# Gates of a bidirectional HGRN2 scan, two units at a time as 2x2 blocks with seven block products, and the scan in three groups of units instead of two

## The chip, the cores and the metric

The kernel runs on one core of one Trainium2 chip. The metric is the device time of one execution in microseconds (us); the time of a kernel is the median of several executions. TensorE (PE) multiplies matrices into PSUM, VectorE (DVE) and ScalarE (ACT) work on the elements, GpSimd (POOL) does small operations, and SyncE (SP) issues most of the DMA transfers.

## The reference

One layer: a bidirectional HGRN2 mixer over 2048 latent tokens behind 256 context tokens, then a gated ConvFFN, both behind a normalisation with adaLN. Width 1024, 8 heads of 128. Cut to the part that the change touches:

```
h = modulate(rmsnorm(x), shift, scale)                    # context and latent tokens
q, zf_fwd, zf_bwd, v, g = split(h @ w_in, 5)              # w_in 1024 x 5120
q = silu(q)
for d, zf in enumerate((zf_fwd, zf_bwd)):
    f = lb[d] + (1 - lb[d]) * sigmoid(zf)                 # the gates
    logf[d], k[d] = log(f), 1 - f
# per head and direction, in chunks of 64 tokens:
# S_t = diag(f_t) S_{t-1} + k_t v_t^T,   o_t = S_t^T q_t
y = (rmsnorm(o_fwd + o_bwd) * silu(g)) @ w_out
```

## The kernel before, in words

**Tiles and units.** Tokens go in tiles of 128: two of context (-2, -1) and sixteen latent ones (0 to 15). Three tiles are a unit of 384 tokens. `GROUPS` has two groups of three units. For a group, the normalised and transposed tokens stand in SBUF, in six places; all eight heads are walked over the group's units, then the next group's tokens take the places.

**Products.** Every operand is split into a high and a low part (`split`, L79 to L81: ACT copies the high part, DVE subtracts), and a product is three matmuls for each of eight slices of the inner dimension (`mm3`, L353 to L358: high x high, high x low, low x high). Per head and unit there are the two gates (`z`, 2 x 24 matmuls of 384 columns), the queries (24 of 384) and the values with the output gate (72 of 256); the first unit, with two context tiles, has other forms of the last two. A head's weights are loaded from w_in as five raw tiles of 0.5 MB (`load_feat`, `load_vg`, L162) and split, in each group anew.

**The scan of a unit** (`unit`, L363). The gates pass a sigmoid on ACT and an affine on DVE (L404). DVE makes running products along the chunks: S (L448) forwards, F (L461) backwards, their reciprocal rt (L463), and from these ke, kd, km of the keys and qp, qe, qm, qi of the queries (L453 to L492). The queries' own gate is q (L440). Each value tile's output gate is st (L424): it reads PSUM, so the value's PSUM buffer is free only behind it. Then, for each of three tiles, `part_a` transposes kd (L542, PSUM buffer "tr") and makes four score matmuls (L550 to L557) that DVE masks (L563 to L566), and `part_b` makes kv and o (L574, L589) and updates the state Sf (L593). These six steps are left in a list, and run between the products of the unit that follows.

**Buffers that matter.** In PSUM the ring "pj" has three buffers, for gates, queries and values in turn. "tr" has one, for the transposes of kd and for those of new tokens (`transpose_mod`, L108 to L119: four blocks on PE, L112, then four `hm` on ACT, L116, or DVE, L119). Tokens of the group that follows are loaded into `xt` (two buffers, `x_tile`), normalised (a square L100, a power on POOL L77, a scaling L103) and transposed, all between the products of the last head.

**What sets the order.** The code's lists give the order in which work is issued to the framework, whose scheduler then sets an order for each engine within the dependences; on the chip each engine keeps it. Between the end of the values of one unit and the gates of the next PE has no other work than this. Other work that is spread in between: the rest of w_ada (`ada_rest`) and, in the last head, the eight steps of the output weights (`out_weight`, L642 is DVE's product in it).

The seven block products are not new to the kernel: its ConvFFN has them, in the lines behind L720. After the scan come the readout with w_out and the ConvFFN; the change leaves both alone.

## Time and profile before

| | |
|---|---|
| median of three runs | 2854.65 us (2854.46 to 2859.17) |
| the profiled execution | 2854.57 us |
| its span, first to last instruction | 2852.8 us |
| mean granted TensorE clock | 0.997 of full speed |
| SP loads of w_in | 80 of 0.5 MB, 3.7 us each to landing |
| loads of new tokens (xt) | 11 of 0.5 MB |
| from HBM, to HBM | 280.65 MB, 101.99 MB |

In the trace's names, out<-in tells what an instruction writes and reads; L is the line of the kernel. A timeline row has the start, the duration, the engine, the line, the operation and its tiles, and in brackets for how long the engine stood idle before it and what ended that. Matmuls overlap, so their pace is read from start to start. A row of groups ends with busy time, the mean of one in ns, and idle time before. The scan runs from about 41 to about 1332 us of the span.

### The profile page before, as it was taken

How to read it: one execution, taken by the hardware profiler on the slowest of the kernel's cores; microseconds unless marked ns; L12 is line 12 of the kernel's file. 1: busy time of each engine (PE TensorE's matmuls, PEld its weight loads, DVE VectorE, ACT ScalarE, POOL GpSimd, SP SyncE). 2: the span in 40 equal slices, each digit the busy share in tenths (PEclk: the TensorE clock that was granted, in tenths of full speed). 3: DMA queues.
4: the chain of work that ended last, by engine and by line, in shares of the span. 5: the costliest groups of instructions: out<-in, count | busy, mean ns of one | idle time of the engine just before them, and what ended most of it. 6: DMA issues, size and time to landing. Idle time of an engine off the chain costs nothing. (4 is left out here: it accounts for less than half of the span.)

```text
span 2852.8 us, 43739 instructions
## 1 busy us (share of the span) xinstructions
PE 2803.9 (98%) x16016; PEld 2503.4 (88%) x16016; DVE 2080.8 (73%) x3698; ACT 1176.5 (41%) x2517; POOL 570.1 (20%) x1020
## 2 busy tenths in 40 slices
PE   7999999999999999998999899999999999999999
PEld 4999999999999999998888688888888888887887
DVE  5766666677667566587898787777887777676887
ACT  5433333355333323333555444444444444333343
POOL 2111111121111111111111243433443342000001
PEclk9999999999999999999999999999999999999999
DMA  6222222222232222135778622225522223987663
GB/s 237 67 79 79 84 76 84 79 78 89 85 90 66 80 78 85 61 98 185 266 293 315 227 86 71 88 82 190 187 89 89 76 73 115 310 301 252 194 200 122
DMA packets 202623, 385.51 MB, mean 135 GB/s; under 512 B 26660, under 2 KB 117796, under 8 KB 197160
## 3 DMA queue, kind: packets, MB, share of 16 engines
q1 hardware_dynamic: 199672, 374.46, 39.1%
q10 hardware_dynamic: 2736, 8.26, 0.8%
q8 instruction: 126, 2.06, 0.3%
q14 instruction: 89, 0.73, 0.1%
HBM read 280.65 MB, written 101.99 MB: 134 GB/s over the span
## 5 line engine op out<-in xcount | busy, mean ns | idle before, releaser
L356 PE MATMUL z<-vh,hh 128*128 128x256 f32 (+1 forms) x1024 | 300.3, 293 | 0.0
L358 PE MATMUL z<-vh,hl 128*128 128x256 f32 (+1 forms) x1024 | 293.4, 287 | 0.0
L357 PE MATMUL z<-vl,hh 128*128 128x256 f32 (+1 forms) x1024 | 293.3, 286 | 0.0
L356 PE MATMUL z<-hh,wh 128*128 128x384 f32 x768 | 264.1, 344 | 0.7 <-ACT hh L80 0.7
L357 PE MATMUL z<-hl,wh 128*128 128x384 f32 x768 | 258.4, 336 | 0.5 <-DVE hl L81 0.5
L358 PE MATMUL z<-hh,wl 128*128 128x384 f32 x768 | 258.7, 337 | 0.0
L1338 PE MATMUL y<-wd,ml 128*128 128x512 f32 x600 | 234.0, 390 | 2.1 <-DVE ml L81 2.1
L1336 PE MATMUL y<-wd,mh 128*128 128x512 f32 x600 | 233.8, 390 | 0.9 <-DVE P L1390 0.7
L1337 PE MATMUL y<-wd,mh 128*128 128x512 f32 x600 | 233.5, 389 | 0.0
L356 PEld LDWEIGHTS z<-vh,hh 128*128 128x128 f32 x1024 | 196.3, 192 | 0.0
L357 PEld LDWEIGHTS z<-vl,hh 128*128 128x128 f32 x1024 | 196.1, 191 | 0.0
L358 PEld LDWEIGHTS z<-vh,hl 128*128 128x128 f32 x1024 | 195.8, 191 | 0.0
L81 DVE TENSOR_TENSOR w<-raw,w 128x512 fp32r<-128x512 f32 x180 | 141.9, 793 | 43.1 <-ACT w L80 41.1
L484 POOL COPY TX<-S 128x3 f32<-128x3 f32 x48 | 14.6, 304 | 792.4 <-DVE S L448 792.4
L80 ACT ACTIVATE w<-raw 128x512 fp32r<-128x512 f32 x180 | 111.8, 629 | 141.2 <-PE zd L741 78.6
L81 DVE TENSOR_TENSOR w<-s,w 128x512 fp32r<-128x512 f32 x126 | 122.3, 976 | 49.4 <-ACT w L80 48.6
L424 DVE TENSOR_TENSOR st<-z,st 128x128 f32<-128x128 f32 x127 | 36.5, 287 | 158.7 <-ACT st L423 158.6
L356 PEld LDWEIGHTS z<-hh,wh 128*128 128x128 f32 x768 | 145.3, 189 | 4.4 <-DVE acc L620 1.7
L419 ACT ACTIVATE v<-z 128x128 f32<-128x128 f32 x128 | 35.4, 277 | 271.1 <-PE z L358 271.1
L357 PEld LDWEIGHTS z<-hl,wh 128*128 128x128 f32 x768 | 145.2, 189 | 0.7 <-DVE hl L81 0.7
L358 PEld LDWEIGHTS z<-hh,wl 128*128 128x128 f32 x768 | 144.7, 188 | 0.0
L738 PE MATMUL zc<-rT,w 128*128 128x512 f32 x352 | 137.1, 389 | 2.7 <-ACT w L80 2.7
(337 smaller groups left out, 8119.8 us busy)
## 6 DMA issues: line engine op xcount, KB each, us to landing
raw<-in_w_up_dram SPq DMA_DIRECT2D x88, 512.0 KB, 3.8
raw<-in_w_in_dram SPq DMA_DIRECT2D x80, 512.0 KB, 3.7
lr<-m SPq DMA_DIRECT2D x49, 512.0 KB, 5.5
m<-r SPq DMA_DIRECT2D x66, 256.0 KB, 4.3
raw<-in_w_ada_dram SPq DMA_DIRECT2D x32, 512.0 KB, 4.5
stash<-st SPq DMA_DIRECT2D x125, 128.0 KB, 1.9
kq<-stash SPq DMA_DIRECT2D x15, 1024.0 KB, 7.4
og<-stash SPq DMA_DIRECT2D x15, 1024.0 KB, 6.3
```

The lines of the kernel that those rows point to most:

```text
L80: act.activation(h, src, AF.Copy)
L81: dve.tensor_tensor(l, src, h.bitcast(F32), OP.subtract)
L356: pe.matmul(o, sh[:, k], mh[:, k], start=k == 0, stop=False)
L357: pe.matmul(o, sh[:, k], ml[:, k], start=False, stop=False)
L358: pe.matmul(o, sl[:, k], mh[:, k], start=False, stop=k == KT - 1)
L419: act.activation(v[:, s], z[:, 0:128], AF.Copy)
L424: dve.tensor_tensor(st[:, 1], z[:, 128:256], st[:, 1], OP.mult)
L484: pool.tensor_copy(TX[:, 0, :, 0], tot[:, 0, :, 1])
L738: pe.matmul(o, w[:, 0, k], r[:, :, 0, k], start=start and k == 0, stop=False, skip_group_check=True)
L1336: pe.matmul(z, lh, rh, start=start, stop=False, skip_group_check=True)
L1337: pe.matmul(z, lh, rl, start=False, stop=False, skip_group_check=True)
L1338: pe.matmul(z, ll, rh, start=False, stop=stop, skip_group_check=True)
```

## The change

**Gates.** Two units a and b make a pair. Their gates are one block product: on the left the weights A (rows: the two directions; columns: the two halves of the inner dimension), on the right the tokens B (rows: the halves; columns: a and b). It is done by seven products of half the depth instead of eight, in the order of the tuple `GATES`, with sums S1 to S4 of weight blocks and T1 to T4 of token blocks; ACT and DVE put the seven together in PSUM and SBUF (`gates`: a copy, and additions at L540, L544, L551, L555, L559). Each product is 12 matmuls of 384 columns. The first unit's two gates are complete behind the fourth and the sixth product, the second unit's behind the fifth and the seventh. The first pair of all is done plainly (`gates_plain`). The affine of the gates is on ACT now (L510).

**Three groups of two units.** A group holds eight right factors (B11 to B22, T1 to T4) in SBUF. Those of groups two and three are made beside the heads of the group before (`prep`, spread by `BESIDE` and `weave`), stored to DRAM (fac_d), and loaded when the places come free (`next_factors`). `xt` has one buffer, which the pieces to be stored and the sums of w_ada also use (tag "xt").

**Weights are split once.** A head's seven left factors (wf_d) and its value and query weights (wv_d) are stored after the first group and loaded in the later ones (`prepare`, four products ahead, five buffers; `vq_weights`, one buffer each).

Counted: the 384-column gate matmuls go from 2304 to 2028; raw loads of w_in from 80 to 42; new are 16 stores and 32 loads of 1.5 MB for wv_d, 56 stores and 112 loads of 0.5 MB for wf_d, 48 stores of 0.5 MB and 16 loads of 1.5 MB for fac_d.

The order is moved with it. On DVE, in a unit of the second half before, the queries' products and the first st follow the one unit's scans:

```order
L563 COPY_PREDICATED AB_434<-mx,sc 128x128
L593 SCALAR_TENSOR_TENSOR Sf<-Sf,sd,kv 128x128
L564 COPY_PREDICATED AB_434<-mb,sc 128x128
L565 COPY_PREDICATED AB_435<-mf,sc 128x128
L467 TENSOR_TENSOR qp<-q,F_430 128x384
L566 TENSOR_TENSOR at<-AB_434,AB_435 128x128
L468 TENSOR_TENSOR qp<-q,F_430 128x384
L492 TENSOR_TENSOR qm<-qp,TX_438 128x3x64
L492 TENSOR_TENSOR qe<-qp,rt 128x768
L492 TENSOR_TENSOR qi<-qp,TB_436 128x768
L492 TENSOR_TENSOR qm<-qp,TX_438 128x3x64
L424 TENSOR_TENSOR st<-z,st 128x128
```

On DVE, in a pair of the third group of the change (F_514 is the first unit's, F_515 the second's; L644 and L652 are the scans S and F, L607 is st):

```order
L644 SCALAR_TENSOR_TENSOR S<-F_515,d_511 128x396
L623 TENSOR_TENSOR q<-z,q 128x384
L644 SCALAR_TENSOR_TENSOR S<-F_515,d_511 128x396
L704 TENSOR_TENSOR qp<-q,F_514 128x384
L705 TENSOR_TENSOR qp<-q,F_514 128x384
L682 TENSOR_TENSOR qm<-qp,TX_522 128x3x64
L682 TENSOR_TENSOR qe<-qp,rt 128x768
L682 TENSOR_TENSOR qm<-qp,TX_522 128x3x64
L682 TENSOR_TENSOR qi<-qp,TB_520 128x768
L652 SCALAR_TENSOR_TENSOR F_515<-F_515,d_511 128x396 x2
L654 RECIPROCAL rt<-S 128x24
L607 TENSOR_TENSOR st<-z,st 128x128 x3
```

The second unit's four scans stand ahead of the first unit's st; ahead of these rows, and behind L559, stand the first unit's four scans, rt, one Sf, ke, kd and km.

On SP, at the start of the third group of the change (fB are right factors, v the value and query weights, wf a left factor; wf0S_148 is the fifth product's, since four are loaded ahead):

```order
L437 DMA fB_10587<-fac2B_142 128x3072
L437 DMA fB_10589<-fac2B_143 128x3072
L476 DMA v_10591<-wv_200 128x3072
L476 DMA v_10592<-wv_201 128x3072
L451 DMA wf<-wf0S_148 128x1024
L451 DMA wf<-wf0A_149 128x1024
L451 DMA wf<-wf0S_150 128x1024
```

On SP between two heads before, loads of raw weights stand among the stores of results:

```order
L162 DMA raw<-in_w_in_dram 128x1024
L602 DMA stash_74<-st 128x128
L601 DMA stash_74<-st 128x256
L162 DMA raw<-in_w_in_dram 128x1024
L602 DMA stash_75<-st 128x128
L601 DMA stash_75<-st 128x256
```

Four transfers of 1.5 MB now stand ahead of the left factor there; in the other heads of groups two and three it is the two of v. And on PE, in a head of the first group of the change, where a new tile is transposed (tp):

```order
L118 MATMUL tp<-ident,xt 128x128 x4
L741 MATMUL sc<-qm,km 128x128
L734 MATMUL sc<-qe,ke 128x128
L735 MATMUL sc<-qe,ke 128x128
L740 MATMUL sc<-qp,kx 128x128
L741 MATMUL sc<-qm,km 128x128
L726 MATMUL tr<-ident,kd 128x128 x4
L758 MATMUL kv<-v,kt 128x128 x2
L726 MATMUL tr<-ident,kd 128x128 x2
L758 MATMUL kv<-v,kt 128x128 x2
L487 MATMUL z<-fB_228,wf 128x384
L489 MATMUL z<-fB_228,wf 128x384
```

The scan's transposes tr follow the tile's tp through the same PSUM buffer; before, in the last head, tp stood between rows of value matmuls:

```order
L358 MATMUL z<-vh,hh_466 128x256
L112 MATMUL tp<-ident,xt 128x128 x4
L356 MATMUL z<-vh,hh_466 128x256
L357 MATMUL z<-vl,hh_466 128x256
L358 MATMUL z<-vh,hl_467 128x256
L356 MATMUL z<-vh,hh_466 128x256
```

The diff, cut to its core:

```diff
 GROUPS = (
-    ((-2, -1, 0), (1, 2, 3), (4, 5, 6)),
-    ((7, 8, 9), (10, 11, 12), (13, 14, 15)),
+    ((-2, -1, 0), (1, 2, 3)),
+    ((4, 5, 6), (7, 8, 9)),
+    ((10, 11, 12), (13, 14, 15)),
 )
+SCAN_A = ((8, 15), (4, 18), (4, 18))
+SCAN_B = (12, 22)
+BESIDE = ((3, 4), (4, 6), (0, 0))
...
+    GATES = (("A11", "B11"), ("S2", "T2"), ("S3", "T3"), ("A12", "B21"), ("S1", "T1"),
+             ("A22", "T4"), ("S4", "B22"))
...
+    def left_tile():
+        return wp.tile([128, 2, 4, 128], F32R, name="wf", tag="wf", bufs=5)
...
+                def put(n, src, i=i):
+                    w = xp.tile([128, 2, 4, 128], F32R, name="w", tag="xt", bufs=1)
+                    split(w[:, 0], w[:, 1], src)
+                    sp.dma_start(fac_d[g - 1][n][:, i], w.bitcast(F32))
...
+        def prepare(i):
...
+            w = lefts[i] = left_tile()
+            if ("f", h) in kept:
+                sp.dma_start(w.bitcast(F32), wf_d[h][n])
+                return
...
+        def vq_weights(g, h):
+            if ("v", h) in kept:
+                w = vq_tiles()
+                for v, d in zip(w, wv_d[h]):
+                    sp.dma_start(v.bitcast(F32), d)
+                return w
...
+        def gate(h, u, d, z=None):
...
+            act.activation(v, z, AF.Sigmoid)
+            j = (1 - d) * NH + h
+            act.activation(v, v, AF.Identity, scale=oml[:, j:j + 1], bias=lb[:, j:j + 1])
...
+            for n, (ln, rn) in enumerate(GATES):
+                prepare(i + n + 4)
+                w, r = lefts.pop(i + n), fac[rn]
+                if n == 0:
+                    z1 = pj()
+                    acc_gate(z1, w, r, True, False)
+                    u2 = gp.tile([128, NS, 32], F32, name="u2", tag="S")
+                    act.activation(u2, segs(z1), AF.Copy)
+                elif n == 1:
+                    z2 = pj()
+                    acc_gate(z2, w, r, True, True)
+                    dve.tensor_tensor(u2, u2, segs(z2), OP.add)
...
+                elif n == 5:
+                    acc_gate(z3, w, r, False, True)
+                    dve.tensor_tensor(gate_view(0, 1), u2, segs(z3), OP.add)
+                    gate(h, 0, 1)
+                else:
+                    acc_gate(z2, w, r, False, True)
+                    dve.tensor_tensor(gate_view(1, 0), u2, segs(z2), OP.add)
+                    gate(h, 1, 0)
...
+                ua.early()
+                ua.queries()
+                drain()
+                ua.late()
+                if not head0:
+                    ub = Unit(h, w, 1, units[1])
+                    ub.early()
+                if last:
+                    weave([lambda k=k: out_weight(k) for k in range(KT)], 0, 40)
+                else:
+                    weave(some(BESIDE[g][1]), 0, 24)
...
+                        ua.values(s)
...
+                weave(ua.scan(), *SCAN_A[g])
+                ub.queries()
+                ub.values(0)
+                ub.values(1)
+                drain()
+                ub.late()
+                ub.values(2)
+                if h == NH - 1 and not last:
+                    next_factors(g + 1, ("B12", "B22"))
+                scan_b = ub.scan()
```

`early` holds a unit's S and F scans, rt and POOL's factors, `late` the products of keys and queries; `weave` and `drain` spread listed steps over the products that follow.

653 lines of the change are left out of this document (396 added, 257 removed).

## The prediction

> **What bounds the kernel now.** I read the page first: its span, then the busy shares.
>
> ```profile
> span 2852.8 us, 43739 instructions
> PE 2803.9 (98%) x16016; PEld 2503.4 (88%) x16016; DVE 2080.8 (73%) x3698; ACT 1176.5 (41%) x2517; POOL 570.1 (20%) x1020
> ```
>
> TensorE (PE) is busy for 98% of the span and VectorE (DVE) for 73%. That is an average, so I asked for PE's waits between 60 and 1420 us, which is the scan and the first tiles behind it (columns: total us, times, longest).
>
> ```profile
> PE kv L574 <- DVE Sf L593: 2.9, 5, 0.7
> PE tr L542 <- DVE hm L119: 1.7, 5, 1.0
> ```
>
> These are the largest two that a line of the scan has: PE is hardly ever kept waiting there. So a matmul that goes is worth its whole spacing, and a new wait costs its whole length. The spacing is read from PE's timeline, start to start, since durations of pipelined matmuls overlap.
>
> ```profile
> 600.67 0.60 PE L112 MATMUL tp<-ident,xt 128*128 128x128 f32 x4
> 601.02 0.42 PE L356 MATMUL z<-hh,wh 128*128 128x384 f32 x1
> ...
> 602.17 0.33 PE L356 MATMUL z<-hh,wh 128*128 128x384 f32 x1
> 602.34 0.33 PE L357 MATMUL z<-hl,wh 128*128 128x384 f32 x1
> 602.52 0.33 PE L358 MATMUL z<-hh,wl 128*128 128x384 f32 x1
> ...
> 702.62 0.38 PE L542 MATMUL tr<-ident,kd 128*128 128x128 f32 x2
> ...
> 703.73 0.61 PE L574 MATMUL kv<-v,kt 128*128 128x128 f32 x4
> ...
> 704.98 0.28 PE L356 MATMUL z<-vh,hh 128*128 128x256 f32 x1
> 705.10 0.28 PE L357 MATMUL z<-vl,hh 128*128 128x256 f32 x1
> ...
> 707.50 0.60 PE L574 MATMUL kv<-v,kt 128*128 128x128 f32 x4
> ...
> 708.31 0.36 PE L356 MATMUL z<-vh,hh 128*128 128x256 f32 x1
> ```
>
> A 384-column matmul takes 0.174 us (two take 0.35, from 602.17 to 602.52; 0.174 over a longer row of them), a 256-column one 0.12 and four transposes of a tile 0.35. A tile's part_a (transposes and four score matmuls, 702.62 to 703.73) takes 1.11 us, its part_b (kv and o) 0.81. What DVE needs behind the gates stands in its timeline of the same head.
>
> ```profile
> 700.17 0.98 DVE L461 TENSOR_TENSOR_SCAN F<-F,d 128x396 f32<-128x396 f32 x1
> 701.07 0.27 DVE L463 RECIPROCAL rt<-S 128x24 f32<-128x24 f32 x1
> 701.26 0.29 DVE L492 TENSOR_TENSOR km<-ke,TX 128x192 f32<-128x192 f32 x1
> 703.10 0.96 DVE L492 TENSOR_TENSOR kd<-ke,TB 128x768 f32<-128x768 f32 x1 [1.55 <-PE tr L542]
> 703.98 0.55 DVE L440 TENSOR_TENSOR q<-z,q 128x384 f32<-128x384 f32 x1
> 704.48 0.30 DVE L563 COPY_PREDICATED AB<-mx,sc 128x128 f32<-128x128 uint32 x1
> ...
> 706.11 0.55 DVE L468 TENSOR_TENSOR qp<-q,F 128x384 f32<-128x384 f32 x1
> 706.58 0.35 DVE L492 TENSOR_TENSOR qm<-qp,TX 128x192 f32<-128x192 f32 x1
> 706.85 0.95 DVE L492 TENSOR_TENSOR qe<-qp,rt 128x768 f32<-128x768 f32 x1
> 707.72 0.95 DVE L492 TENSOR_TENSOR qi<-qp,TB 128x768 f32<-128x768 f32 x1
> 708.59 0.35 DVE L492 TENSOR_TENSOR qm<-qp,TX 128x192 f32<-128x192 f32 x1
> 708.86 0.28 DVE L424 TENSOR_TENSOR st<-z,st 128x128 f32<-128x128 f32 x1
> 709.06 0.33 DVE L593 SCALAR_TENSOR_TENSOR Sf<-Sf,sd,kv 128x128 f32<-128x128 f32 x1
> 711.94 0.29 DVE L424 TENSOR_TENSOR st<-z,st 128x128 f32<-128x128 f32 x1 [2.55 <-ACT st L423]
> ```
>
> Start to start: an F scan 0.90 (an S scan has the same size and is taken alike), rt 0.19, kd 0.88, q 0.50, qp 0.47, qm 0.27, qe and qi 0.87, st 0.20. The last row shows the slack: DVE stood idle for 2.55 us before the second st, so it was ahead of PE. One unit's chain fits behind PE; the change puts two units' chains in one place.
>
> **The change part by part.** The sum is made against the profiled execution: 2854.57 us, of which the span is 2852.8; the median of the three runs, 2854.65, is the same within 0.1 us.
>
> *Matmuls removed.* The gates of a pair of units take 84 instead of 96 matmuls of 384 columns, for 23 of the 24 pairs (the first stays plain): 276 x 0.174 = **48.0 us** off PE. As PE sets the pace, all of it counts. The transposes only change place. The five additions that DVE gains per pair at 0.50 (q's row) are 2.5 us against four gate affines that go to ACT.
>
> *The wait behind the last product.* The three PSUM buffers of the ring "pj" are shared by the gates, queries and values. The second unit's queries need the buffer of the first unit's first values, which frees with its st product; in DVE's new order that st stands behind the scans of both units. From the last product: the addition L559 (0.50), four S scans and four F scans (7.20), two rt (0.38), Sf (0.27, as qm), two ke (1.00, as q), two km (0.54), kd 0.88, q 0.50, two qp 0.94, two qm 0.54, qe and qi 1.74, st 0.20: 14.7 us. Beside it PE has the first unit's queries (24 x 0.174 = 4.18), its values (72 x 0.12 = 8.58) and one part_b (0.81): 13.6 us. With about 0.3 for two hand-overs, an estimate (ACT's copy of a value starts 0.2 behind PE's next instruction:
>
> ```profile
> 707.70 0.28 ACT L419 ACTIVATE v<-z 128x128 f32<-128x128 f32 x1 [2.60 <-PE z L358]
> ```
>
> against 707.50), PE waits 1.4 us per pair. The bounds are 0 (a tenth less on DVE) and 3.2 (each instruction at its full duration rather than its spacing: 16.5 us in all). Group 2 and group 3 have 8 pairs each: 16 x 1.4 = **+22.4**. In the first group other work stands between, and I count nothing.
>
> *Stored weights loaded again.* In groups 2 and 3 a head's two value tiles (1.57 MB each) go ahead of the fifth product's left factor (0.52 MB) on SP's queue, and can start only when the last values of the head before are done. Rates and latencies, by a window at the start, and the groups and issues that a tile's preparation has:
>
> ```profile
> 15.00:25.00 10.00, 10.00 (x24) 1.96 (x23) 1.65 (x3) 1.31 (x3) 1.70 (x7) 1.00 1.02 410
> ```
>
> ```profile
> L116 ACT ACTIVATE hm<-tp,B,A 128x128 f32<-128x128 f32 x200 | 74.1, 465 | 65.0 <-PE tp L112 64.1 <-DVE A L224 0.9
> L77 POOL TENSOR_TENSOR rs<-rs,mhalf 128x1 f32<-128x1 f32 x34 | 22.9, 677 | 205.0 <-DVE rs L76 200.8 <-issue 3.6 <-DVE B L698 0.5
> L103 ACT ACTIVATE xt<-xt,rs 128x1024 f32<-128x1024 f32 x11 | 12.7, 1153 | 12.6 <-POOL rs L77 12.6
> L100 ACT ACTIVATE junk<-xt 128x1024 f32<-128x1024 f32 x11 | 11.7, 1060 | 5.0 <-DMA xt<-in_x_dram 5.0
> L642 DVE SCALAR_TENSOR_TENSOR raw<-raw,vec,g 128x1024 f32<-128x1024 f32 x8 | 10.1, 1270 | 0.0
> ```
>
> ```profile
> xt<-in_x_dram SPq DMA_DIRECT2D x11, 512.0 KB, 3.9
> ```
>
> The window's last column is 410 GB/s. A load of 0.52 MB needs 1.3 us of that and landed after 3.9, so about 2.6 is latency. The 3.67 MB take 8.95 us, and land after 9.0 to 11.6; four products (48 x 0.174 = 8.35) and two part_a (2.2) make the factor due at 10.6. The wait lies between 0 and 1.0; I take 0.5, the middle, for 14 heads: **+7**. The page "DMA: Bandwidth & Descriptors" of the Trainium skill (Specifications) limits one core's HBM traffic to about 358 GB/s; the trace moved 410, so the measurement decides. By 358 these loads would be 1.3 us later in each of the 14 heads, an estimate of +18 more.
>
> *Right factors made beside.* A tile's x has one buffer now, and its four-block transposes use the one buffer "tr" that the scan's transposes have too. In four heads of the first group: a transpose of four blocks (0.35) and four hm (1.86) until tr is free, the second transpose 0.35, then the next x: load 3.9, square 1.06, power 0.68, scale 1.15. That is 9.35 us until the third transpose. PE has about 6.7 in between (three part_a 3.3, kv and o 1.7, two transposes 0.7, five gate matmuls 0.9, a value 0.1): 2.7 of wait, 4 x 2.7 = 10.8. The transposes that follow each other behind some 1.7 us of matmuls wait 0.5 more, eight times: 4. Together **+15**, between 0 (the planner's order covers it) and 22 (half the small matmuls run ahead).
>
> *Between groups.* SP loads B12, B22 and the two value tiles (6.3 MB) and then the fifth left factor: 6.82 MB / 410 = 16.6, with latency 19.2, against 10.6 due: 8.6 us; I take 8 at each of the two changes, since the first of these loads may start early: **+16** (0 to 2 x 15, if the stores ahead of them are still running). A wait of this kind has a second price in the clock:
>
> ```profile
> 49.57 1.12 PE L112 MATMUL tp<-ident,x 128*128 128x128 f32 x4 [4.93 <-DVE x L105]
> 50.34 0.67 PE L356 MATMUL z<-hh,wh 128*128 128x384 f32 x1
> ...
> 54.33 0.38 PE L356 MATMUL z<-hh,wh 128*128 128x384 f32 x1
> ```
>
> After 4.93 us without work twelve matmuls took 3.99 us (50.34 to 54.33) instead of 2.09, and the transposes 0.77 instead of 0.35: 2.3 us lost. Two such waits: **+4.6**. The page "TensorE: Matmul & The Clock Gate" of the Trainium skill (Part 1: The HAM clock gate) puts the limit at about 3.4 us without work and the return at as long again of work; the trace agrees on the return (4 us), and shows no wait that tests the limit from below. By it the waits of 2.7 cost no clock, and a little longer ones would cost 2.3 each.
>
> *Start and end.* The wait of 4.93 gets 27 instead of 12 matmuls ahead of it: -15 x 0.174 = -2.6. The eight out_weight steps lie in one pair instead of three units: each 1.27 on DVE and a split of about as much, 20 us; a pair takes PE 52 us (132 matmuls of 0.174, 144 of 0.12, six times part_a and part_b), and DVE's 73% of it (38) and 20 pass that by 6, and with their bunching I take 7.6. Together **+5**.
>
> Sum: -48.0 + 22.4 + 7 + 15 + 16 + 4.6 + 5 = +22: **2877 us**, with its own range 2862 to 2895 (half of the walk's waits either way).
>
> **The rivals.**
>
> *A, on the other side: the scan stays bound by PE.* The place is the stretch between L559 and the second unit's queries. DVE's chain is longer than PE's cover by only 1.4 in 14.7; if it runs a tenth shorter (ACT or POOL take parts earlier, scans start before L559 as the first unit's gates are done by the sixth product) the 22.4 go, and with a DVE that keeps up the 7 and the 15 go too. Then -48.0 + 16 + 4.6 + 5 = -22: **2832 us** (2818 to 2848). For it speaks that DVE idled 2.55 us at this place before; against it that the order puts all eight scans behind L559. The point from which it decides: the waits of a pair, over 23 pairs, below about 1 us.
>
> *B, it cancels.* Half of the walk's 44 us of waits are real: 2877 - 22 = **2855**.
>
> *C, the chain at full durations.* If the rows that follow each other don't overlap as they did, each of the 16 pairs waits 3.2 instead of 1.4: +29, **2906 us** (2895 to 2930). For it: PSUM and SBUF are shared with more traffic from stores and loads; against it: the spacings above are from a busy stretch.
>
> **How the numbers follow.** Forecast 0.42, A 0.30, B 0.10, C 0.18. The range takes A down to 2822 and C up to 2925. About 0.2% (5.7 us) is what a measurement of this kernel can tell from no change. A is faster (0.30), B the same (0.10), the forecast and C slower (0.60).
>
> **What would show it.** Right: in the profile after, the waits list has PE waiting for st at the second unit's queries, some 1.4 us in each pair of groups 2 and 3, for the load of wf, and for xt in the first group; two waits of about 8 us stand at the group changes, with the clock low behind them; PE's share falls to some 96%. Wrong: hardly a wait at L559's stretch and pairs of groups 2 and 3 that are 2.1 us shorter than two units of before (then A), or waits there of 3 us (C), or a wait at an engine that I gave none, ACT above all, which takes the affine and the stores' splits.

## The result, and the profile after

The changed kernel takes 2970.93 us (median of 4 runs, 2966.04 to 2971.84), the kernel before, in the same runs, 2856.91 (2854.46 to 2859.41): a ratio of 1.0396 (95% interval 1.0378 to 1.0414), 114 us slower. I had forecast slower, but by 22 us and not over 2925. First the page of the changed kernel: its span and the busy shares.

```profile
span 2968.4 us, 43955 instructions
PE 2815.1 (95%) x15740; PEld 2492.1 (84%) x15740; DVE 2134.7 (72%) x3776; ACT 1268.4 (43%) x2725; POOL 649.3 (22%) x1020
```

PE has fewer matmuls, is yet busy for longer, and its share fell from 98% to 95%. Where it happened shows in the first matmul of the readout, the first work behind the scan, in PE's timeline of before and then of after:

```profile
1327.12 1.95 PE L858 MATMUL oi<-Sb,kq 128*128 128x128 f32 x16
```

```profile
1442.90 2.50 PE L1120 MATMUL oi<-Sb,kq 128*128 128x128 f32 x10 [4.40 <-DMA kq<-stash]
```

The scan ends 115.8 us later, the whole span 115.6: all of it lies in the scan. So in what follows I compare where the scan ends (1442.9 for the change). Busy time by stretch tells waiting from slowness; the whole scan, before and then after, and under it the scan of after in stretches (seven pairs of the first group, its last head with the change of group, the second group, most of the third). The columns are the stretch, its length, busy time of PE, PEld, DVE, ACT and POOL, the granted clock, and the DMA share and rate.

```profile
41.50:1327.10 1285.60, 1271.17 (x9088) 1253.00 (x9089) 866.51 (x1950) 484.23 (x1425) 197.19 (x593) 1.00 0.26 81
```

```profile
41.50:1442.90 1401.40, 1284.11 (x8841) 1241.64 (x8841) 921.58 (x2036) 577.92 (x1636) 271.28 (x590) 0.97 0.59 211
...
69.30:452.90 383.60, 347.41 (x2312) 332.84 (x2312) 285.81 (x629) 218.15 (x554) 80.86 (x177) 0.97 0.63 231
452.90:522.90 70.00, 51.84 (x306) 48.82 (x305) 38.10 (x86) 22.43 (x61) 9.99 (x26) 0.85 0.87 331
522.90:1016.40 493.50, 456.11 (x3150) 437.93 (x3151) 310.01 (x669) 176.34 (x527) 92.43 (x197) 0.97 0.66 233
1016.40:1400.00 383.60, 373.23 (x2724) 370.56 (x2723) 231.72 (x538) 127.95 (x407) 77.80 (x178) 1.00 0.42 151
```

PE stands idle for 117.3 us of the scan (1401.4 - 1284.1) instead of 14.4: 103 more. It is busy 13 us longer though 48 us of matmuls are gone: what is left takes 61 us more. Part of that is the clock, 0.97 of full speed in the first two groups and 0.85 at the change of group. The record of the granted clock has 119 us at half speed in the whole run, and 22 before; about 94 of the 119 are in the scan, 15 of them on idle time, so half of the other 79, some 40 us, is pace lost; before loses 2 to 3 us in its scan in the same way, which leaves 37. Of the other 24 us most are the edges of the waits. In the rows under e2 the last matmul ahead of a wait is shown for 0.28 us where its neighbours follow 0.12 apart, and the first one behind it is followed after 0.29 instead of 0.174: PE is shown busy there, but 0.25 us of pace are lost, in the mean over the change's waits. The change has 106 waits of 0.05 us and more in the scan and before has 20, so this makes some 21 us.

The third group, which has nothing beside it, runs at full clock and waits little; the loss is in the groups that make something else meanwhile. The waits of PE from the start to behind the scan (total us, times, longest), where before had 2.9 as its largest line of the scan:

```profile
PE z L583 <- DVE st L607: 22.1, 15, 3.3
PE tp L118 <- ACT xt L109: 17.3, 7, 3.5
PE kv L758 <- DVE Sf L766: 7.7, 1, 7.7
PE sc L734 <- DVE AB L749: 6.7, 5, 3.5
...
PE sc L734 <- DVE qe L682: 6.1, 6, 2.3
PE kv L758 <- DVE Sf L777: 5.8, 12, 1.5
PE kv L758 <- DVE Sf L764: 5.3, 4, 1.3
...
PE z L585 <- DMA v<-wv: 5.1, 2, 3.9
...
PE z L487 <- DMA fB<-fac1B: 3.5, 2, 3.1
```

The first line is the wait that I forecast behind the last product, the second the wait for xt. The two lines with DMA are loads at the changes of group, and the 7.7 is a store there (e8). The others are new and short, for VectorE's ordinary steps of the scan (Sf, AB, qe), waits to which the prediction gave nothing.

### The profile page after: what moved, and what is told of

Its sections match the earlier page's. It is cut to its first block, busy times and chain, and to the rows that moved or that the text cites. A ratio compares the mean times of both kernels' runs of the same rounds, so it can differ in the third digit from the quotient of the medians.

```text
span 2968.4 us, 43955 instructions
## 1 busy us (share of the span) xinstructions
PE 2815.1 (95%) x15740; PEld 2492.1 (84%) x15740; DVE 2134.7 (72%) x3776; ACT 1268.4 (43%) x2725; POOL 649.3 (22%) x1020
## 4 chain that ended last, share of the span: by engine, by line
PE 57%; DVE 9%; DMA 8%; POOL 2%; issue 2%; ACT 1%; SPq 0%; DVEq 0%; POOLq 0%; ACTq 0%
PE y L1600 3%; PE y L1598 3%; PE y L1599 3%; PE zc L1000 3%; PE zc L1003 3%; PE zc L1002 3%; PE za L1000 3%; PE zd L1000 3%; PE zd L1003 3%; PE za L1003 3%; PE zd L1002 3%; PE za L1002 3%; PE z L487 2%; PE z L491 2%; PE z L489 2%; PE z L594 2%
## 5 line engine op out<-in xcount | busy, mean ns | idle before, releaser
L594 PE MATMUL z<-v,fB 128*128 128x256 f32 (+1 forms) x1024 | 300.2, 293 | 2.1 <-ACT v L86 2.1
L595 PE MATMUL z<-v,fB 128*128 128x256 f32 (+1 forms) x1024 | 294.6, 288 | 2.9 <-DVE v L87 2.7
L596 PE MATMUL z<-v,fB 128*128 128x256 f32 (+1 forms) x1024 | 293.7, 287 | 0.0
L669 POOL COPY TX<-S 128x3 f32<-128x3 f32 x48 | 31.7, 659 | 939.6 <-DVE S L644 939.6
L594 PEld LDWEIGHTS z<-v,fB 128*128 128x128 f32 x1024 | 195.8, 191 | 5.3 <-ACT v L86 3.5
L595 PEld LDWEIGHTS z<-v,fB 128*128 128x128 f32 x1024 | 195.8, 191 | 4.4 <-DVE v L87 4.4
L596 PEld LDWEIGHTS z<-v,fB 128*128 128x128 f32 x1024 | 195.8, 191 | 0.0
L583 PE MATMUL z<-fB,v 128*128 128x384 f32 (+1 forms) x384 | 133.6, 348 | 22.5 <-DVE st L607 22.1
L83 POOL TENSOR_TENSOR rs<-rs,mhalf 128x1 f32<-128x1 f32 (+1 forms) x50 | 57.2, 1143 | 375.0 <-DVE rs L82 368.0
L1000 PE MATMUL zc<-rT,w 128*128 128x512 f32 x352 | 137.0, 389 | 2.1 <-DVE uv L1485 2.1
L86 ACT ACTIVATE w<-s 128x512 fp32r<-128x512 f32 x126 | 78.4, 628 | 137.2 <-POOL s L1056 76.7
L1002 PE MATMUL zc<-rT,w 128*128 128x512 f32 x352 | 136.9, 389 | 0.0
L1003 PE MATMUL zc<-rT,w 128*128 128x512 f32 x352 | 136.9, 389 | 0.0
L1600 PEld LDWEIGHTS y<-wd,ml 128*128 128x128 f32 x600 | 112.6, 188 | 26.5 <-DVE ml L87 3.2
L585 PE MATMUL z<-fB,v 128*128 128x384 f32 (+1 forms) x384 | 129.7, 338 | 5.1 <-DMA v<-wv 5.1
L1598 PEld LDWEIGHTS y<-wd,mh 128*128 128x128 f32 x600 | 112.6, 188 | 24.9 <-ACT X L1633 1.6
```

Of the source, the lines that this page charges most:

```text
L86: act.activation(h, src, AF.Copy)
L583: pe.matmul(z, wh[:, k], self.tok(k, 0, s), start=k == 0, stop=False)
L594: pe.matmul(z, th, wh[:, k, 0:n], start=k == 0, stop=False)
L595: pe.matmul(z, th, wl[:, k, 0:n], start=False, stop=False)
L596: pe.matmul(z, tl, wh[:, k, 0:n], start=False, stop=k == KT - 1)
L1000: pe.matmul(o, w[:, 0, k], r[:, :, 0, k], start=start and k == 0, stop=False, skip_group_check=True)
```

## The experiments

Most runs stand for a part of the change that is undone or made lighter. The median is against 2970.93, the ratio against the kernel before in the same runs; "behind" is the span less the scan's end (1525.5 in the change, 1525.7 before).

| run | median us | ratio (95%) | scan ends | behind |
|---|---|---|---|---|
| e1_eighth | 3006.12 | 1.0517 (1.0499 to 1.0534) | 1484.4 | 1532.5 |
| e2_st_ahead | 2949.51 | 1.0319 (1.0304 to 1.0334) | 1419.4 | 1529.7 |
| e3_ada_off_dve | 2990.00 | 1.0464 (1.0449 to 1.0480) | 1462.2 | 1527.0 |
| e4_two_x | 2949.15 | 1.0316 (1.0301 to 1.0332) | 1417.0 | 1524.8 |
| e5_ada_spread | 2964.55 | 1.0371 (1.0349 to 1.0393) | 1435.4 | 1529.6 |
| e6_filler | 2977.83 | 1.0418 (1.0397 to 1.0439) | 1445.1 | 1529.1 |
| e7_together | 2932.75 | 1.0262 (1.0243 to 1.0281) | 1403.7 | 1525.3 |
| e8_stores_on_act | 2975.21 | 1.0411 (1.0383 to 1.0439) | 1439.7 | 1525.0 |
| e9_warm_power | 3005.95 | 1.0511 (1.0486 to 1.0536) | 1445.6 | 1562.2 |
| e10_one_scan_more | 2975.91 | 1.0414 (1.0388 to 1.0439) | 1446.9 | 1526.3 |
| e11_no_ada_sums | 2942.84 | 1.0298 (1.0272 to 1.0325) | 1413.6 | 1522.8 |
| e12_together_2 | 2958.34 | 1.0348 (1.0326 to 1.0371) | 1396.1 | 1559.7 |
| e13_no_new_tiles | 2907.09 | 1.0180 (1.0163 to 1.0197) | 1377.0 | 1526.9 |
| e14_four_bytes | 3003.12 | 1.0511 (1.0490 to 1.0532) | 1441.6 | 1559.9 |
| e15_sixty_four_bytes | 2997.72 | 1.0492 (1.0471 to 1.0513) | 1441.6 | 1553.7 |
| e16_row_broken | 2956.80 | 1.0354 (1.0334 to 1.0374) | 1430.6 | 1523.2 |

### The gain and the walk: e2 and e1

e2 moves the second unit's scans behind the first unit's values in the order of the code, so that st no longer stands behind them.

```diff
-                    ub.early()
...
                         ua.values(s)
+                if not head0:
+                    ub.early()
```

> The second unit's scans are issued behind the first unit's values; on DVE the first st then stands ahead of two of the second unit's four scans, 1.8 us earlier. Theory (the wait of the second unit's queries for st is real and is this chain): the third group's pairs go from 53.8 to about 52.5 us, and the whole from 2971 to about 2955 (12 to 19 us less). Rival (the chain only moves: the second unit's kd and part_a are late instead): no change, 2971.

The scan ends 23.5 us earlier. One wait of the third group in the change, with the matmuls beside it, and then a pair of that group (from one rt to the next) in the change and in e2:

```profile
1080.75 0.28 PE L596 MATMUL z<-v,fB 128*128 128x256 f32 x1
1082.27 0.45 PE L583 MATMUL z<-fB,v 128*128 128x384 f32 x1 [1.24 <-DVE st L607]
1082.56 0.34 PE L584 MATMUL z<-fB,v 128*128 128x384 f32 x1
```

```profile
1125.26:1179.02 53.76, 52.52 (x386) 52.15 (x385) 31.98 (x76) 17.62 (x57) 10.94 (x25) 1.00 0.43 155
```

```profile
1122.17:1174.43 52.26, 52.26 (x386) 52.09 (x385) 31.96 (x76) 17.65 (x57) 10.97 (x25) 1.00 0.45 162
```

PE has no idle time in e2's pair: 52.26 us where two units of before, in heads with nothing beside, took 54.4 in the mean. So the 2.1 us per pair are there in the third group, and the wait behind the last product is as deduced. The pair is 1.50 us shorter, for a wait of 1.24: the edges are the rest.

e1 makes the second product twice, so that the eighth one is back.

```diff
                     acc_gate(z2, w, r, True, True)
+                    acc_gate(z2, w, r, True, True)
```

> The second product (S2 by T2) is made twice in each of the 23 pairs, 276 matmuls of 384 columns more, with the same result. Theory (PE sets the pace wherever it isn't waiting, so the seven products did save their 48 us and the loss is elsewhere): 276 x 0.174 = 48 us more, about 3019. Rival (the stretch of the gates is bound by DVE, ACT or the loads, so the eighth product had cost little and the change never saved its 48): 0 to 25 us more.

It cost 41.5 us in the scan of the profiled execution, which is the longest of e1's four (3018.57; the median is 35 us above the change). That it is near the 48 of 23 times 12 matmuls is chance: 28 of the 41.5 are in seven pairs of the third group, twice what the matmuls cost there, and 13 in the sixteen pairs ahead of them, where the matmuls alone are 33. So in the first two groups, where PE waits for others, the eighth product had cost less than its length, and the theory holds for the third group only. There a pair became 58.3 instead of 53.8: 2.1 are the matmuls, 0.95 a longer wait at st (2.19 for 1.24; why it grew I don't know), and 1.5 are the clock: in one pair the wait was cut into about 1.8 and 0.4 by the edge of two clock windows, and this pair took 56.8. In e1's timeline of PE matmuls behind the whole wait run 0.32 apart instead of 0.174, and a table in windows of 3.41 us (the length of the clock record's pieces) shows why.

```profile
1098.46 0.44 PE L584 MATMUL z<-fB,v 128*128 128x384 f32 x1 [2.19 <-DVE st L608]
...
1100.07 0.52 PE L585 MATMUL z<-fB,v 128*128 128x384 f32 x1
1100.39 0.52 PE L586 MATMUL z<-fB,v 128*128 128x384 f32 x1
```

```profile
1096.07:1099.49 3.42, 1.23 (x8) 1.03 (x7) 2.73 (x7) 0.45 (x2) 3.36 (x12) 0.99 0.09 24
1099.49:1102.90 3.41, 3.41 (x13) 3.31 (x12) 0.00 (x0) 0.00 (x0) 0.01 (x1) 0.51 0.00 0
```

All 2.19 us are idle inside one window, and the next window has half the clock.

### The clock: e10 and all the records

e10 makes the first S scan of the second unit twice in the third group, so that the wait grows by a scan.

```diff
-                for d in range(2):
+                for d in (0, 0, 1) if tiles[0] == 13 else (0, 1):
```

> In the third group's eight heads the second unit's first S scan is made twice, with the same result: 0.9 us more of DVE ahead of st, so PE's wait there grows from 1.2 to 2.1 us and nothing else changes. Theory of the clock by windows (a stretch of 3.4 us in which PE idles for 2 us or more is followed by one at half the clock, one with less than 1.5 us is not): 0.9 and some 1.5 us for the clock, pairs of 53.8 become 56 or more in most heads, 16 to 20 us in all. Rival (the clock falls only after 3.4 us without any work): pairs of 54.7, 7 us in all.

The wait grew to 2.09 us and the pairs to 54.6, which is the rival's time: in six of the eight pairs the clock stayed at 1.00. A pair of 54.6 us is 16 windows of 3.41, so the wait meets the windows at the same place each time; the stretches on both sides of that boundary:

```profile
1076.10:1079.51 3.41, 3.02 (x26) 2.81 (x24) 3.41 (x6) 0.80 (x4) 0.39 (x1) 1.00 0.07 20
1079.51:1082.92 3.41, 1.72 (x10) 1.72 (x11) 2.03 (x6) 0.09 (x1) 2.53 (x10) 1.00 0.14 40
1082.92:1086.33 3.41, 3.41 (x25) 3.37 (x24) 0.57 (x3) 0.82 (x3) 0.00 (x0) 1.00 0.02 5
```

The wait is cut into 0.4 and 1.7, and no window falls. So e10 doesn't decide between the two; e1's windows above do, where 2.19 us were enough, and a count does: over the change and the experiments e1 to e13, all windows at full speed from 41.5 us to the end of the scan, by PE's idle time within one.

| idle in a window, us | under 1.5 | 1.5 to 1.7 | 1.7 to 2.0 | 2.0 to 3.4 |
|---|---|---|---|---|
| windows | 5022 | 46 | 67 | 176 |
| followed by half speed | 0 | 5 | 45 | 176 |

Behind the scan two windows with 1.3 and 1.5 us idle fell as well (in e1 and e8), so the limit isn't sharp. It isn't the length of a wait that counts but whether about half of a window is idle. The profile before had shown it already, in the ConvFFN: in its timeline of PE and in two windows, a wait of 2.84 us is followed by half the clock.

```profile
1600.65 0.76 PE L738 MATMUL zd<-rB,w 128*128 128x512 f32 x1 [2.84 <-DVE uv L1219]
```

```profile
1597.24:1600.66 3.42, 0.58 (x4) 0.19 (x2) 3.42 (x7) 1.54 (x3) 0.00 (x0) 1.00 1.05 447
1600.66:1604.07 3.41, 3.41 (x8) 2.73 (x9) 0.45 (x1) 0.00 (x0) 0.00 (x0) 0.50 0.93 394
```

And its wait of 3.42 us at 1332.48, which an edge cuts (1.9 and 1.8 us idle in the two windows), is followed by none. The page "TensorE: Matmul & The Clock Gate" of the Trainium skill (Part 1: The HAM clock gate) has the free-running window of 3413 ns, and these records agree; it asks for about 3.4 us without work for the fall, and there the measurement decides: from 2.0 us within one window the clock fell every time.

e6 was to test this the other way: twelve matmuls without a use ahead of the second tile's transposes, to fill the wait for xt.

```diff
+        for _ in range(fill):
+            pe.matmul(tp[:, 0, :], ident, ident, start=True, stop=True)
```

> Before the transposes of each second tile, twelve matmuls of the identity by itself go into their own PSUM buffer, with no effect on the result: PE works for some 2.6 us in a wait of 3.4 that it has anyway, in six heads. Theory (the waits of 3.4 us also halve the clock for 3.4 to 6.8 us, and a shorter stretch without work doesn't): the four long pairs of the first group fall by 1.5 to 3 us each, the whole by 6 to 15 us, though more matmuls run. Rival (the clock is low for other reasons): 0 to 10 us more.

The waits of 3.4 us stayed as they were, since they belong to the first tile's transposes, not the second's: a miss, which tells nothing of the clock, but shows that my place for the xt wait was wrong.

### The wait for xt: e4, e9 and e16

e4 gives the second tile of a head a buffer of its own, so that the chain from the second transpose to the next x is gone.

```diff
-                    hms.append([x_tile(xp, t), hm_tile(f"hm{c}")])
+                    hm = hm_tile(f"hm{c}")
+                    flat = hm.rearrange("p k n -> p (k n)")
+                    if c == 0:
+                        xt, junk = x_tile(xp, t), flat
+                    else:
+                        xt = x_tile(xp, t, xt=flat)
```

> A second tile's x is loaded into its own hm buffer, at the same time as the first one's, instead of after the first one's transposes. Theory (the third transpose waits 3.4 us for its x in four heads of the first group and two of the second, and each of these waits also halves the clock for 3.4 to 6.8 us): 4 x (3.4 + 3) and 5 more, 30 us less, about 2940. Rival (the wait alone counts, and the clock is low for other reasons): 17 us less, about 2954.

The scan ends 25.9 us earlier and the waits for xt fall from 17.3 to 7.8 us in total, but one of 3.4 is left. This is not the chain from the second transpose: in the first group no wait for xt of the change is at a second tile, all are at a head's first one. In the change the wait of this kind in PE's timeline, and the power that the tile's scaling needs, on POOL:

```profile
207.01 1.11 PE L118 MATMUL tp<-ident,xt 128*128 128x128 f32 x4 [3.36 <-ACT xt L109]
```

```profile
202.25 3.53 POOL L83 TENSOR_TENSOR rs<-rs,mhalf 128x1 f32<-128x1 f32 x1 [9.53 <-DVE rs L82]
218.06 0.54 POOL L83 TENSOR_TENSOR rs<-rs,mhalf 128x1 f32<-128x1 f32 x1 [12.28 <-DVE rs L82]
```

One column takes 3.53 us at one place and 0.54 at another. It is slow at 202.25, 308.35 and 412.76, in three of the heads, and the waits of 3.4 are there. In e4 they stand at other places of VectorE's work: two of the three powers take 0.54 and their waits are 0.50, and the third takes 3.53 and its wait is 3.37. My first guess was code that must be fetched; e9 makes a power of another column on POOL just ahead.

```diff
+                    pool.tensor_tensor(idle, TBs[1][:, 0, 0, 3:4], mhalf[:, 0:1], OP.pow)
```

> Before each new tile's square, POOL makes one power more, into a tile that nobody reads, right behind its work for the unit before; that is some 9 us ahead of the power that the tile needs. Theory (that power takes 3.5 us in three heads of the first group because POOL has not run one for 90 us, and is the wait of 3.4 us that PE has there): in these heads the power takes 0.5 to 0.9, the wait goes below 1 us, and the clock stays up: 3 x (3 + 2), 10 to 18 us less, about 2956. Rival (the power is slow for what runs beside it, or the wait has another end): 2971, with 3.5 us as before.

The added powers took 0.54, the tile's own still 3.54: not the code. What lies beside it is VectorE's row of the second unit's queries, here the first instruction behind the power's start and the last one, of seven that follow each other:

```profile
202.29 0.55 DVE L705 TENSOR_TENSOR qp<-q,F 128x384 f32<-128x384 f32 x1
...
204.70 0.68 DVE L87 TENSOR_TENSOR wf<-s,wf 128x512 fp32r<-128x512 f32 x1
```

Each reads two SBUF tiles. The row ends at 205.38 and the power at 205.78, 0.40 later; it is 0.39 at the two other places. e16 puts an instruction that reads nothing into that row.

```diff
                 qe = self.qe = gp.tile([128, 2, NS, 32], F32, name="qe", tag="qe")
+                if self.tiles[-1] < 4:
+                    dve.memset(qe[:, 0, s0 * 4:s0 * 4 + 1, 0:4], 0.0)
```

> In the heads of the first group, a memset of four columns is put on VectorE between the second unit's products qp and qm. In the profile of the change the three slow powers on POOL (3.52 to 3.53 us instead of 0.54, at 202.25, 308.35 and 412.76) all start beside a row of VectorE products that read two SBUF tiles each and follow each other without a gap, and all end 0.39 to 0.40 us behind the end of that row; the memset reads nothing and stands 0.5 us behind the power's start. Theory (POOL's power gets no turn at SBUF while VectorE's products of two SBUF tiles follow each other): the power ends some 0.4 us behind the memset's start, so it takes 1.0 to 1.3 us; the wait of PE for xt in these three heads falls from 3.4 to about 1 us, and with the half-speed windows behind it the scan ends 7 to 13 us earlier, at 1430 to 1436. Rival (something else slows the power there, as its place in POOL's own sequence): it stays 3.5 us, the waits of 3.4 stay, and the scan ends within 4 us of 1442.9.

In e16's timelines, the power on POOL, the memset on DVE and the first tile's transposes on PE:

```profile
203.44 0.98 POOL L83 TENSOR_TENSOR rs<-rs,mhalf 128x1 f32<-128x1 f32 x1 [9.54 <-DVE rs L82]
```

```profile
203.97 0.06 DVE L710 MEMSET qe<- 128x4 f32 x1
```

```profile
205.65 0.66 PE L118 MATMUL tp<-ident,xt 128*128 128x128 f32 x4 [0.82 <-ACT xt L109]
```

The power ends at 204.42, 0.45 behind the memset's start, and takes 0.98 us in all three heads; the wait of 3.36 is 0.82, the waits for xt fall from 17.3 to 7.3 us in all, and the scan ends 12.3 us earlier. (The half-speed time of the whole run didn't fall with it, 123 us for 119.) So it is a lock-out by VectorE's unbroken row, and the rival fell. The page "SBUF — State Buffer" of the Trainium skill (SBUF: two separate sides) says that a VectorE instruction with two SBUF inputs and a GpSimd instruction that reads SBUF exclude each other for an instruction's whole length; the trace agrees, and shows that POOL gets no turn between instructions that follow each other either.

### What is made beside the scan: e13, e11, e5 and e3

e13 leaves the preparation of the new tiles out.

```diff
-                    hms.append([x_tile(xp, t), hm_tile(f"hm{c}")])
-                    xt, hm = hms[-1]
-                    normalize(xt, hm.rearrange("p k n -> p (k n)"), xp, on_act=True)
+                    hms.append([None, hm_tile(f"hm{c}")])
+                    pool.memset(hms[-1][1], 1.0)
...
-                    xt, hm = hms[c]
-                    transpose_mod(xt, hm, half, ps, *mods(t), "tr", 1, True)
+                    return
```

> Leaves out the loads, norms and transposes of the new tiles in the first and second group: the right factors of groups two and three are made of ones, with the same sums, splits, stores and loads. Theory (in the first group the new tiles' chain from load to transposes, with the clock behind its waits, is most of what every second pair takes longer): the pairs of 57 to 58 us there fall to about 49, those of the second group by 3 to 5 where tiles were made, 40 to 50 us less, about 2925. Rival (the splits and stores beside, and the weights that are split and stored, make the first group slow): 10 us less.

The scan ends 65.9 us earlier. The first group's seven pairs of e13 stand against the row of 383.60 above:

```profile
69.90:411.53 341.63, 325.16 (x2258) 317.10 (x2258) 287.56 (x622) 178.01 (x467) 70.53 (x178) 1.00 0.69 250
```

42 us less with the clock at 1.00 and 16.5 us idle instead of 36.2, while DVE is as busy as before. So it isn't that DVE has too much to do, but the waits in the heads with new tiles and the clock behind them: those for xt (12 us in these pairs), and four of 1.32 for Sf, four of 0.5 to 0.8 for kt and three for hm, which e13 hardly has. It takes the tiles' loads and their work on ACT and POOL away with them, so it doesn't say which of these delays Sf and kt. Some 8 us of the 65.9 are the transposes' own time on PE (12 tiles, two rows of 0.35 each), which the kernel before spends too.

e11 leaves out the loads and sums of w_ada that are spread over three pairs of the second group.

```diff
-                raw = rawp.tile([128, D], F32, name="raw", tag="raw")
-                sp.dma_start(raw, a["w_ada"][k * 128:(k + 1) * 128, c:c + D])
...
+                if k == 0:
+                    sp.dma_start(acc[i], a["w_ada"][0:128, c:c + D])
```

> Leaves out the products and sums of the rest of w_ada (31 of 32 loads and all 32 DVE steps); the rows that later parts read are made of one slice alone, by the same matmuls at the same places. Theory (the three pairs of 62 to 66 us are long for these steps on DVE and the clock behind the waits they cause): these pairs fall to 55 or 56, 25 to 30 us less in all, about 2943; the kernel before spent nothing on these steps, since PE did not wait for them. Rival (the loads and stores of the second group make it slow): 5 us less at most.

29.3 us less, 20.5 of it in those three pairs (64.9, 62.5 and 65.5 became 58.7, 55.0 and 58.7). The second of them in the change, then in e11:

```profile
775.10:837.60 62.50, 56.48 (x390) 53.57 (x389) 43.00 (x87) 18.78 (x59) 11.88 (x25) 0.97 0.67 219
```

```profile
759.88:814.89 55.01, 54.59 (x390) 52.35 (x389) 32.24 (x77) 18.80 (x59) 10.93 (x25) 1.00 0.46 162
```

PE waits 6.0 us with ten such sums beside (43.0 - 32.2 = 10.8 us of DVE), and 0.4 without, and the clock comes back. The run takes 31 loads away too, but these aren't what PE waits for: in the three pairs of the change its only wait for a load is one of 1.4 us for wf; the others are for DVE and ACT. The sums stand in DVE's order between the three st, each 1.19 us long:

```profile
722.06 0.28 DVE L607 TENSOR_TENSOR st<-z,st 128x128 f32<-128x128 f32 x1
722.26 1.27 DVE L811 SCALAR_TENSOR_TENSOR acc<-raw,sil,acc 128x1024 f32<-128x1024 f32 x1
723.45 0.28 DVE L607 TENSOR_TENSOR st<-z,st 128x128 f32<-128x128 f32 x1
```

e5 spreads the same sums thinner, over the third group too.

```diff
-BESIDE = ((3, 4), (4, 6), (0, 0))
+BESIDE = ((3, 4), (2, 4), (1, 1))
```

> The same steps of the rest of w_ada, on DVE as in the change, but at most six steps of work beside in a pair of the second group and two in one of the third, instead of ten in the second group and none in the third. Theory (ten steps in a pair put 13 us of DVE work among the chain that PE waits for; two steps find room in the 25% that DVE is idle): the three pairs of 62 to 66 us fall to about 56, the third group's rise by 1 to 2 us each, the whole to about 2945 to 2955. Rival (each step costs PE its 1.28 us and the share of clock wherever it lies): 2971, the third group's pairs 3 us longer.

7.5 us less in the scan: the three long pairs fell to 55 to 60, but the pair of the second change of group rose from 59.9 to 67.0 and the third group's to as much as 58.3, and half-speed time rose from 119 to 142 us. So spreading the sums moved most of the loss to other places.

e3 takes the sums off DVE: the product on ACT, the addition on POOL.

```diff
+                    act.activation(raw, raw, AF.Copy, scale=sil[:, k:k + 1])
+                    pool.tensor_tensor(acc[i], acc[i], raw, OP.add)
```

> The 32 steps of the rest of w_ada, which now lie in the second group's last five heads, are scaled on ACT and added on POOL instead of one DVE instruction of 1.28 us each. Theory (these steps stand in DVE's queue between the parts that PE waits for, and each such wait also lowers the clock): those five pairs come down from 60 to 65 us to about 55, the whole to about 2940 (25 to 35 us less). Rival (the second group is slow because of its loads and stores): no change within 5 us.

19.3 us more. The sum on POOL is late for those who need it, as its list of PE's waits shows:

```profile
PE z L818 <- POOL acc L812: 15.5, 3, 6.5
```

So it moved the wait instead of taking it away, and doesn't tell what the sums cost on DVE.

### The change of group: e8

The longest wait, 7.7 us at the first change of group, is no load of a factor. kv waits for Sf, which waits for ACT's copy kb, which waits for a store of the stash (the results that go to DRAM):

```profile
489.83 0.28 ACT L761 ACTIVATE kb<-kv 128x128 f32<-128x128 f32 x1 [6.42 <-DMA stash<-st]
```

e8 puts the last head's stores on ACT's queue, past the loads of factors on SP's.

```diff
-                q_ = act if h == NH - 1 and t > NT - 4 else sp
+                q_ = act if h == NH - 1 else sp
```

> In the last head of each group the stores of results go to ACT's queue, so that they don't stand behind the loads of right factors on SP's. Theory (the wait of 7.7 us at the first change of groups is a store that waits on SP's queue behind factor loads which wait for their places, with the buffers of st full): that pair of 70 us falls by 7.7 and its share of clock, 8 to 12 us less in all, about 2960. Rival (ACT's queue then waits for the same transfers): no change.

The wait stays, in e8's timeline of PE:

```profile
490.06 1.23 PE L758 MATMUL kv<-v,kt 128*128 128x128 f32 x4 [8.40 <-DVE Sf L766]
```

But the edit doesn't reach the store in question. It belongs to the head before the last, whose last steps run in this pair, and so SP still issues it. In SP's timeline of the change and then of e8 it stands behind two loads of 1.5 MB:

```profile
476.05 2.36 SPq L437 DMA_DIRECT2D fT<-fac1T  x2
478.47 0.47 SPq L785 DMA_DIRECT2D stash<-st  x1
```

```profile
474.83 2.38 SPq L437 DMA_DIRECT2D fT<-fac1T  x2
477.27 0.47 SPq L785 DMA_DIRECT2D stash<-st  x1
```

In the change it was issued at 478.47 and landed 11.1 us later, at 489.56; the copy kb starts at 489.83. In the record of the transfers the packets of the two loads, 3.1 MB, fill the time from 479 to 488 us, and the store's own move in the microsecond behind them. e13, with the same two loads ahead of the same store, has 9.01 us at this place. So the store waits for the transfers ahead of it on its queue, which is near to the theory, and e8 doesn't speak against it. This is read from the traces; no run has moved the store.

### Together, and a tile of four bytes: e7, e12, e14 and e15

e7 has e2, e4, e5 and e8 at once; e12 has e2, e4, e5 and e9.

> The second unit's scans behind the first unit's values, the second tile's x in its hm buffer, the w_ada steps spread to the third group, and the last heads' stores on ACT's queue, all at once. Theory (the losses are separate, and add up): 21 + 22 + 20 + 8 us less than 2971, about 2900; that is still above the kernel before, and the third group's pairs stay near 53. Rival (the chain through DVE only moves from one place to the next): 2930 or more.

> As the four changes together, without the stores on ACT's queue and with the extra powers. Theory (what is left in the first group is DVE's and ACT's work beside, not one transfer or one power): 2920 to 2930, still 2 to 3 per cent above the kernel before. Rival (the power was the rest of the first group's loss): below 2905.

e7 is 38 us faster than the change (2932.75) and still 2.6% slower than the kernel before: the 71 of the theory didn't come, and the time is the rival's. The four alone had given 45 us by their medians (21.4, 21.8 and 6.4, and e8 4.3 more), so the sizes were too large, and the losses overlap besides. e12 missed its forecast, by what lies behind the scan: its scan ends earlier still than e7's, at 1396.1, but 34 us are lost behind it; e9 had lost 37 there too. Both have one tile more, a column of four bytes per partition. e14 and e15 are the change with an unused tile, of four and of 64 bytes.

```diff
     mhalf = small("mhalf")
+    unused = small("unused", (128, 1))
+    pool.memset(unused, 1.0)
```

> One tile of one number per partition more is allocated ahead of all others, as in the run with extra powers, and used by nothing. Theory (that run's extra 36 us behind the scan came from the addresses, which all move by four bytes): the scan keeps its time, and the ConvFFN's products take 2 to 3 per cent longer, 3005. Rival (they came from the powers): 2971.

> The same with sixteen numbers per partition. Theory (the addresses matter by where they fall within 64 bytes): 2971, as without the tile. Rival (any move counts): 3005.

32 and 27 us slower, all of it behind the scan, so not only a shift by four bytes does it, but also one by 64. In PE's timeline of the ConvFFN, of the change and then of e14, matmuls of 512 columns are in the median 0.227 apart and 0.234:

```profile
1899.66 0.39 PE L1002 MATMUL zb<-rT,w 128*128 128x512 f32 x1
1899.88 0.39 PE L1003 MATMUL zb<-rT,w 128*128 128x512 f32 x1
```

```profile
1899.61 0.40 PE L1002 MATMUL za<-rB,w 128*128 128x512 f32 x1
1899.84 0.40 PE L1004 MATMUL za<-rB,w 128*128 128x512 f32 x1
```

The change itself doesn't pay this (1525.5 behind the scan against 1525.7), so it is no part of the 114 us. That the addresses do it is argued, since all that the runs add is the tile and its memset; which tile's place matters I haven't tried.

## Why the prediction was wrong in its size

| term of the sum | forecast us | measured us |
|---|---|---|
| matmuls removed | -48.0 | -48 by count (2.1 per pair shown in the third group, e2) |
| wait behind the last product | +22.4 | 22.1 (15 waits) |
| stored weights late | +7 | 3.6 (waits for wf) |
| new tiles: waits for xt | +15 | 17.3 |
| changes of group | +16 | 9.4 of loads and 7.7 of a store |
| clock | +4.6 | about 37 |
| other waits of PE in the scan | 0 | about 43 (103 new idle less 60 named; 4.4 of it the readout's first load) |
| pace lost at the edges of waits, and rest | 0 | about 24 (some 21 at the edges) |

The start and end (+5) I can't set apart from these lines; all lines but that one make 116.

*Right.* The direction and its mechanism: PE no longer stays fed, because both units' scans stand ahead of the first unit's st. The wait is 1.24 us in six of the third group's eight pairs, where I took 1.4, and e2 takes it away. Rival A is out (the named waits of the walk, 43 us, are 1.9 us a pair, not below 1), and so are B, no change, and C (3.2 in each pair). C's ground isn't seen either: with the DMA share at 0.63 instead of 0.26 a product qe still takes 0.87 us start to start (203.03 to 203.90).

*Near by chance, the sums of waits.* The waits that I named make about 60 us, and I had 60.4. But the 22.1 at st are six of 1.24, two of 2.9 and 3.3 in the third group, four of 0.4 to 3.1 in the second and three short ones in the first, not 16 of 1.4.

*Wrong, the clock.* The step "Two such waits: +4.6" priced the clock at the two longest waits alone, from one row, a wait of 4.93. I wrote that the trace shows no wait that tests the limit from below, and took zero for all waits of 1 to 3.4 us. That was misread: the profile before has the wait of 2.84 with half the clock behind it. Between 1.5 and 2.0 us within a window the fall begins. With 37 us the clock is one of the two largest terms after the gain, and it comes on top of each medium wait: with it a wait of 2.2 costs 3.7.

*Wrong, the price of a wait.* The step "a new wait costs its whole length" left out its edges, 0.25 us for each, some 21 us in all.

*Wrong, the work beside the scan.* "In the first group other work stands between, and I count nothing", and the w_ada steps did not stand in the sum at all, since before had them too. Before, DVE had slack (idle for 2.55 us ahead of st), which the change uses up. e13 and e11 together give 95 us of the 116 in the scan, some 8 of it work that before has as well; the effects may overlap, so they aren't to be added up exactly. Most of the other waits of 43 us, and a part of the clock, are these.

*Right by chance, the wait for xt.* Its size was near (17.3 for 15), but my chain, from a second transpose to the next x, made none of it in the first group. There the waits are at the first tiles, three of them 3.36 behind the slow power (e16 takes 10 of the 17.3 away), for which my chain had 0.68 instead of 3.5. In the second group, 3.5 are at the first tile behind the change of group.

*Off, the group changes.* The first costs 15.5 (fB 3.5, v 4.3, Sf 7.7) where I had 8, the second 1.6 (v 1.2, wf 0.4); and the largest part waits for a store behind two loads, not for the fifth left factor.

Open: how the waits for Sf and kt beside new tiles divide among ACT, DVE and POOL, which no run takes apart, and what is left of the first group's waits without new tiles (16.5 us in seven pairs).

## What to carry to other kernels

A change that takes work off the engine that sets the pace, and puts the helper's work nearer to it, should be priced by the helper's slack at the place, with all that runs beside it there, also what the kernel had already. Price a wait by its edges and by the clock's window, not by its length alone: one of 2.2 us cost 3.7, the same cut in two by the window's edge cost 2.2. Before a run is taken to settle where a transfer waits, see that its edit reaches that transfer. The mean of a group of cheap instructions can hide the one that matters (0.68 for a power of 3.5).

## What the runs showed of the hardware

Four things I had not expected. From 2.0 us of idle within one window of 3.41 us of the scan TensorE had half the clock in the next one, 176 times of 176; under 1.5 never in 5022. Each wait cost it 0.25 us more than it stood idle. A one-column power on POOL waited out a row of seven VectorE instructions (3.53 us instead of 0.54), and a memset of 0.06 us in that row let it through after 0.98. And an unused tile of four or 64 bytes per partition went with matmuls far from there that were 3% slower (0.234 for 0.227 us apart, 27 to 32 us per run).
